# A list-scheduled transformer block: other latencies in the plan, and the mixer's x loaded earlier

## The chip, the cores and the metric

One Trainium2 chip, all eight NeuronCores. Each core computes one sequence of the batch with the same program. The metric is the device time of the slowest core, in microseconds. A program on all eight cores sometimes runs in a slower state, in which one die (cores 0 to 3 or 4 to 7), or both, is granted a lower TensorE clock.

## The reference

```python
def reference(x, c, ...):                       # x (8, 4096, 1024), c (8, 1024), float32
    mod = silu(c) @ w_mod + b_mod               # 9 modulation vectors a sequence
    h = ada_rmsnorm(x, g_ffn1, sh1, sc1)
    x = x + 0.5 * gt1 * swiglu_ffn(h)           # FFN 1: 1024 -> 2 x 2816 -> 1024
    h = ada_rmsnorm(x, g_mix, sh2, sc2)
    u_val, u_gate, u_x, u_y = split(h @ w_in)   # 4 x 512 channels
    y_conv = silu(layernorm(causal_conv31(u_val * sigmoid(u_gate))))
    y_rnn  = gelu(u_y) * rg_lru(causal_conv4(u_x))      # linear recurrence along the sequence
    x = x + gt2 * (concat(y_conv, y_rnn) @ w_out)
    h = ada_rmsnorm(x, g_ffn2, sh3, sc3)
    x = x + 0.5 * gt3 * swiglu_ffn(h)           # FFN 2
    return ada_rmsnorm(x, g_final, f_shift, f_scale)
```

## The kernel before

The sequence is cut into eight tiles of 512 tokens. The first 900 us run FFN 1, in four pairs of tiles. The rest runs mixer and FFN 2 tile by tile, and x goes through memory between the two phases (`xmid`). The instructions are not written in the order in which they run: every operation is added to a list with an estimated duration, a priority and its dependences, and a list scheduler (a greedy simulation on the host) decides the order on each engine, and which buffer each value takes. The program is then emitted in that order. The real semaphore waits come from the dependences, so a wrong estimate can't make the result wrong; it only makes the order a worse one.

The parts that matter here, with cuts marked:

```python
DMA_LAT = 2.0
SEM_LAT = 0.08
# ... schedule(): of the ready operations, the one of best priority that can start now ...
            else:                                  # a DMA
                c = max(s + dur, chan[0]) + op.nbytes
                chan[0] = c
                op.end = c + DMA_LAT               # when the plan thinks that it has landed
        else:
            op.end = s + sw + dur + SEM_LAT        # when the plan lets a dependent one start
# ...
        for q in op.succ:
            q.ready = max(q.ready, op.end if op in q.deps else s)
# ...
        def mix_ffn2(t):
            P.prio = 1000 + 10 * t if t else MIX0
            gate_op = (last_in, anchors[-2][1])[t] if t < 2 else ffn_anchor[t - 2]
            xs = load_x(xm_dr, t, after=(gate_op,) * 8)        # issued when gate_op starts
            hb = norm(xs, ...)                                 # row statistics: matmuls with "ones"
            # ... the four channel groups of the recurrent branch, on VectorE:
                    tsc(b, ux[c][:, 0:T], ...)                 # short convolution, tap 0
                    for k in range(1, 4):
                        stt(b, ux[c][:, k:k + T], ..., b, ...) # taps 1 to 3: each needs the last
            # ... gated linear unit: VectorE frees the PSUM bank of gv
                        stt(ub_t[...], s, 1.0, bv, ALU.add, ALU.mult, ...)
            # ... gate matmuls (need free banks), convolution, output projection w_out ...
            for j in range(FC):                                # FFN 2, 22 slabs of w2i
                slab = load_slab("w2i", j, False)
                ops = ffn_in(slab, [hb2], [hid], j)
            ffn_anchor[t] = ops[-1]                            # x of tile t + 2 is gated on this
            # ... FFN out; for tile 0 its w2o weights are cast to bf16 on first use:
                    slabs = [load_slab("w2o", 3 * q + s, t == 0 and cs.start == 0) for s in range(3)]
```

On VectorE and ScalarE the emitted program waits on the engine's own semaphore too, where an instruction needs the result of an earlier one of the same engine.

## Time and profile before

| what | value | where it is read |
|---|---|---|
| time | 2409.84 us median of 3 (2408.78 to 2412.9) | device times |
| span of the cores | 2386.8 to 2405.7 us | spans of all cores |
| TensorE (PE) busy, slowest core | 2318.5 us, 96% | the page, part 1 |
| PE idle, 61 us to the end of the matmuls | about 24 us | gaps in PE's timeline |

The page of the kernel before: first the busy time, share and number of instructions of each engine, then the chain of work that ended last, by engine.

```profile
PE 2318.5 (96%) x11346; PEld 1110.4 (46%) x11346; DVE 1183.6 (49%) x2019; ACT 931.4 (39%) x1394; POOL 111.2 (5%) x213
...
PE 87%; DMA 6%; ACT 3%; DVE 2%; issue 2%; SPq 1%; ACTq 0%; DVEq 0%; POOLq 0%
```

PE, busy 96% of the span, is the bound, so only its idle time and its granted clock can be won. Who PE waits for (view of the waits, engine PE; microseconds in total, times, longest; waits at the start and for weights left out):

```profile
PE ps L443 <- DVE sb_h L423: 37.0, 15, 12.4
...
PE ps L443 <- DVE sb_c L409: 4.3, 6, 0.8
...
PE ps L443 <- DVE sb_ub L419: 0.5, 1, 0.5
```

Of the 37.0 us behind `DVE sb_h`, which are the row statistics' inputs, some 19 us lie at the start of the program and 3.1 us near 216 us, where pair 1 waits for its x; 7.2 us are these two waits of tile 2's mixer (PE's timeline; start, duration, instruction, and in brackets the idle time before it and what ended it):

```profile
1190.42 0.59 PE L443 MATMUL ps<-sb_h,sb_ones 128*128 128x512 bf16 x1 [4.95 <-DVE sb_h L423]
...
1195.80 0.59 PE L443 MATMUL ps<-sb_h,sb_ones 128*128 128x512 bf16 x1 [2.23 <-DVE sb_h L423]
```

The clock falls with it: the record of core 0 has it at 0.5 for 10.2 us from 1189.2 us. Two stretches of 20 us of the windows view (the length; busy time and number for PE, weight loads, DVE, ACT, POOL; then PEclk, the granted clock; DMA share; GB/s):

```profile
1180.00:1200.00 20.00, 12.81 (x45) 4.87 (x44) 7.64 (x13) 8.68 (x13) 0.53 (x1) 0.74 0.97 282
1240.00:1260.00 20.00, 19.82 (x127) 12.17 (x126) 18.26 (x33) 16.74 (x28) 0.58 (x2) 1.00 1.02 228
```

In the first, PE is granted 0.74 of its clock. And the x loads of the mixer are waited for (view of the tile `xmid`, 1100 to 2200 us):

```profile
L450 SPq DMA_DIRECT2D sb_c<-xmid x48: 319/325/2065, 1178.3 to 2062.9; - x48
...
who waited for it (us, times):
  ACT sb_c L401: 35.1, 13
...
DMA to landing us min/median/max: 3.8/5.4/11.2
```

### The profile page before, as it was taken

The numbers are of one execution on the slowest core, as the hardware profiler recorded it, in microseconds if no ns is written. First come the engines' busy times: TensorE is split into PE (matmuls) and PEld (weight loads), VectorE is DVE, ScalarE is ACT, GpSimd is POOL, SyncE is SP. The second block draws the span as 40 slices with busy tenths as digits, with TensorE's granted clock in tenths as the row PEclk, the third lists the DMA queues.
The fourth block names the chain that finished last, engine by engine and source line by source line (L and its number), as shares of the span: only waits on it lengthen the run. The fifth ranks groups of instructions, "written<-read, shape, count | busy, mean of one in ns | idle before, by whom it ended". The sixth has DMA issues, their size and how long they took to land.

```text
span 2405.7 us, 35029 instructions; the slowest of 8 cores (2386.8 to 2405.7 us)
## 1 busy us (share of the span) xinstructions
PE 2318.5 (96%) x11346; PEld 1110.4 (46%) x11346; DVE 1183.6 (49%) x2019; ACT 931.4 (39%) x1394; POOL 111.2 (5%) x213
## 2 busy tenths in 40 slices
PE   1999999999999999999899999999999999999997
PEld 0444444444444445454354454454454454454446
DVE  6334133523352337585285385484484584574223
ACT  3214011401131116466265365364364364374222
POOL 0010100010010000000000000000000000000000
PEclk9999999999999999999999999999999999999999
DMA  9999599679867766464976555555555555555455
GB/s 274 226 210 240 176 218 220 166 197 221 218 173 188 187 178 206 153 214 149 225 187 221 189 180 188 187 181 185 191 177 191 186 183 185 186 182 188 162 184 184
DMA packets 135106, 466.64 MB, mean 194 GB/s; under 512 B 16368, under 2 KB 18544, under 8 KB 134256
## 3 DMA queue, kind: packets, MB, share of 16 engines
q1 hardware_dynamic: 117216, 386.54, 49.7%
q0 software_dynamic: 17712, 77.87, 17.3%
q8 instruction: 95, 1.56, 0.3%
q14 instruction: 83, 0.68, 0.1%
HBM read 453.07 MB, written 79.69 MB: 221 GB/s over the span
## 4 chain that ended last, share of the span: by engine, by line
PE 87%; DMA 6%; ACT 3%; DVE 2%; issue 2%; SPq 1%; ACTq 0%; DVEq 0%; POOLq 0%
PE ps L443 87%; DMA sb_c<-x 2%; ACT sb_c L401 2%; DMA sb_c<-xmid 2%; SPq L450 1%; DMA sb_slab<-wmod 1%; DVE sb_c L423 1%; DMA sb_slab<-w1i 0%; DVE sb_c L749 0%; DVE sb_c L409 0%; ACT L401 0%; DVE sb_h L423 0%; DVE sb_c L419 0%; DVE sb_ub L419 0%; DVE sb_c L429 0%
## 5 line engine op out<-in xcount | busy, mean ns | idle before, releaser
L443 PE MATMUL ps<-sb_h,sb_slab 128*128 128x512 bf16 (+1 forms) x10160 | 2178.2, 376 | 31.8 <-ACT sb_h L401 28.9
L443 PEld LDWEIGHTS ps<-sb_h,sb_slab 128*128 128x128 bf16 x10160 | 995.9, 98 | 1195.9 <-issue 44.6
L423 DVE TENSOR_TENSOR sb_h<-ps,sb_c 128x512 bf16<-128x512 f32 x352 | 241.4, 691 | 769.4 <-PE ps L443 708.6
L401 ACT ACTIVATE sb_c<-ps 128x512 f32<-128x512 f32 x400 | 236.5, 596 | 868.0 <-PE ps L443 864.5
L423 DVE TENSOR_TENSOR sb_c<-sb_c 128x512 f32<-128x512 f32 (+1 forms) x492 | 308.8, 672 | 115.6 <-ACT sb_c L401 113.0
L401 ACT ACTIVATE sb_c<-sb_c 128x512 f32<-128x512 f32 (+1 forms) x329 | 198.5, 616 | 263.0 <-DVE sb_c L419 183.3
L401 ACT ACT_TABLE_LOAD x106 | 136.0, 1283 | 224.7 <-PE ps L443 202.4
L419 DVE SCALAR_TENSOR_TENSOR sb_c<-ps,sb_gth,sb_c 128x512 f32<-128x512 f32 (+1 forms) x136 | 96.7, 717 | 212.0 <-PE ps L443 211.6
L401 ACT ACTIVATE sb_h<-sb_c,sb_modv,sb_gs 128x512 bf16<-128x512 f32 x151 | 108.9, 801 | 38.5 <-DVE sb_modv L423 24.9
L443 PE MATMUL ps<-sb_ub,sb_slab 128*128 128x256 bf16 x1024 | 115.0, 273 | 4.9 <-DVE sb_c L409 4.3
L443 PEld LDWEIGHTS ps<-sb_ub,sb_slab 128*128 128x128 bf16 x1024 | 99.5, 98 | 22.1 <-issue 8.7
L500 DVE SCALAR_TENSOR_TENSOR sb_slab<-sb_slab,sb_crow 128x1024 f32<-128x1024 f32 x88 | 107.1, 1217 | 3.4 <-DMA sb_slab<-wmod 2.4
L450 POOL DMA_DIRECT2D y<-sb_c x56 | 30.3, 542 | 1012.9 <-ACT sb_c L401 864.1
L423 DVE TENSOR_TENSOR sb_h<-sb_c 128x512 bf16<-128x512 f32 (+1 forms) x98 | 65.8, 678 | 21.8 <-ACT sb_c L401 19.6
L419 DVE SCALAR_TENSOR_TENSOR sb_c<-sb_ux,sb_vecs,sb_c 128x512 f32<-128x512 f32 x96 | 69.6, 746 | 1.7
L443 PE MATMUL ps<-sb_h,sb_ones 128*128 128x512 bf16 (+1 forms) x98 | 34.4, 382 | 37.3 <-DVE sb_h L423 37.0
L419 DVE SCALAR_TENSOR_TENSOR sb_c<-ps,sb_modv,sb_c 128x512 f32<-128x512 f32 x64 | 47.9, 749 | 31.0 <-PE ps L443 31.0
L419 DVE SCALAR_TENSOR_TENSOR sb_ub<-sb_c,ps 64x256 bf16<-64x256 f32 x128 | 53.8, 420 | 15.1 <-PE ps L443 11.6
L450 POOL DMA_DIRECT2D xmid<-sb_c x64 | 35.0, 547 | 361.6 <-DVE sb_c L419 357.8
L401 ACT ACTIVATE sb_c<-sb_c,sb_lam 128x512 f32<-128x512 f32 x64 | 50.0, 821 | 0.5
L409 DVE TENSOR_SCALAR sb_c<-ps,sb_vecs 64x256 f32<-64x256 f32 x85 | 40.7, 484 | 8.9 <-ACT sb_c L401 4.7
L401 ACT ACTIVATE sb_c<-sb_c,sb_modv,sb_gs 128x512 f32<-128x512 f32 (+1 forms) x65 | 43.6, 751 | 1.2 <-DVE sb_c L423 1.2
(50 smaller groups left out, 454.8 us busy)
## 6 DMA issues: line engine op xcount, KB each, us to landing
sb_slab<-b_w2i SPq DMA_DIRECT2D x176, 512.0 KB, 3.8
sb_slab<-b_w2o SPq DMA_DIRECT2D x96, 512.0 KB, 4.0
sb_slab<-wmod SPq DMA_DIRECT2D x88, 512.0 KB, 8.0
sb_slab<-b_w1i SPq DMA_DIRECT2D x66, 512.0 KB, 8.4
sb_slab<-b_win SPq DMA_DIRECT2D x64, 512.0 KB, 4.4
sb_slab<-b_dcw SPq DMA_DIRECT2D x64, 512.0 KB, 3.8
sb_slab<-b_w1o SPq DMA_DIRECT2D x36, 512.0 KB, 5.8
sb_c<-x SPq DMA_DIRECT2D x64, 256.0 KB, 11.2
```

What stands on the lines that cost most here:

```text
L401: return A("ACT", dur, lambda: (lambda o, i: (lambda h: [h.activation(out=o, in_=i, func=func, bias=bias, scale=scale)]))(out(), in_()), r ...
L409: f = lambda: (lambda o, a: (lambda h: [h.tensor_scalar(out=o, in0=a, scalar1=s1, scalar2=s2, op0=op0, op1=op1)]))(out(), in0())
L419: return A("DVE", dur, lambda: (lambda o, a, b: (lambda h: [h.scalar_tensor_tensor(out=o, in0=a, scalar=scalar, in1=b, op0=op0, op1=op1)]) ...
L423: return A("DVE", dur, lambda: (lambda o, a, b: (lambda h: [h.tensor_tensor(out=o, in0=a, in1=b, op=op)]))(out(), in0(), in1()), reads, wr ...
L443: return [h.matmul(o, lhsT=l, rhs=r, start=(first and i == 0), stop=(last and i == n - 1)) for i, (l, r) in enumerate(pr)]
L450: lambda: (lambda o, i: (lambda h: [h.dma_start(out=o, in_=i)]))(out(), in_()),
L500: return lambda h: [h.scalar_tensor_tensor(out=w, in0=w, scalar=1.0, in1=crow.ap, op0=ALU.mult, op1=ALU.mult, accum_out=o)]
```

## The change

Its intent: plan with a longer semaphore latency between engines (0.2 us) and almost none on one engine (0.02 us), plan the mixer's x with 8 us of latency, and issue its load from the 13th of the 22 FFN-in slabs of two tiles back instead of the last one.

```diff
-SEM_LAT = 0.08
+SEM_LAT = 0.2
...
-                op.end = c + DMA_LAT
+                op.end = c + op.lat                       # DMA_LAT unless given
...
-            q.ready = max(q.ready, op.end if op in q.deps else s)
+            t = s if op not in q.deps else op.end - SEM_LAT + 0.02 if op.on == q.eng and not op.nbytes and q.alt is None else op.end
+            q.ready = max(q.ready, t)
...
-            xs = load_x(xm_dr, t, after=(gate_op,) * 8)
+            xs = load_x(xm_dr, t, after=(gate_op,) * 8, lat=8.0)
...
                 ops = ffn_in(slab, [hb2], [hid], j)
-            ffn_anchor[t] = ops[-1]
+                if j == 12:
+                    ffn_anchor[t] = ops[-1]
```

(The rest of the diff passes `lat` through.) No arithmetic is added or taken away.

More of the change, by code (lines that the diff above doesn't have):

```diff
@@ L159, in res @@
         return self.fres if self.pool is None else self.pool.res[self.slot]
+DMA_LAT = 2.0
 class Op:
     __slots__ = ("eng", "dur", "fn", "reads", "writes", "prio", "tset", "deps", "succ", "ndep", "ready",
-                 "idx", "nbytes", "sem", "slab", "end", "after", "sync", "tok", "alt", "on")
+                 "idx", "nbytes", "sem", "slab", "end", "after", "sync", "tok", "alt", "on", "lat")
     def __init__(self):
@@ L176, in __init__, with add @@
         self.prio = 0
-    def add(self, eng, dur, fn, reads=(), writes=(), tset=None, nbytes=0, sem=None, slab=None, after=(), prio=None, sync=(), alt=None):
+    def add(self, eng, dur, fn, reads=(), writes=(), tset=None, nbytes=0, sem=None, slab=None, after=(), prio=None, sync=(), alt=None, lat=DMA_LAT):
         op = Op()
+        op.lat = lat
         op.alt = alt
@@ L207 @@
 D_CAST, D_SLAB, D_CHUNK, D_PREP = 2.7, 1.65, 0.85, 4.6
-DMA_LAT = 2.0
-SEM_LAT = 0.08
+SEM_LAT = 0.2
 SWITCH = 1.4
@@ L446, in mms, with dma @@
             return A("PE", mm_us(n, cols), f, reads, [bank], prio=prio)
-        def dma(q, out, in_, nbytes, sem, reads, writes, slab=None, after=(), prio=None, sync=()):
+        def dma(q, out, in_, nbytes, sem, reads, writes, slab=None, after=(), prio=None, sync=(), lat=DMA_LAT):
             return A(q, 0.06 if q == "SP" else 0.3,
                      lambda: (lambda o, i: (lambda h: [h.dma_start(out=o, in_=i)]))(out(), in_()),
-                     reads, writes, nbytes=nbytes, sem=sem, slab=slab, after=after, prio=prio, sync=sync)
+                     reads, writes, nbytes=nbytes, sem=sem, slab=slab, after=after, prio=prio, sync=sync, lat=lat)
         dr = lambda d, r: d[r * 128:(r + 1) * 128, :]
@@ L523, in build_program, with load_x @@
         tsc(k_(bah.ap), k_(V[:, V_BA:V_BA + 8]), 0.5, None, ALU.mult, None, [vecs], [bah], dur=0.17)
-        def load_x(src, t, prio=None, after=(None,) * 8):
+        def load_x(src, t, prio=None, after=(None,) * 8, lat=DMA_LAT):
             xs = []
@@ L530, in load_x @@
                 d = src[t][f]
-                dma("SP", lambda b=b: b.ap, lambda d=d: d.ap, D_CHUNK, slot_sem(b), [d], [b], prio=prio, after=(after[f],))
+                dma("SP", lambda b=b: b.ap, lambda d=d: d.ap, D_CHUNK, slot_sem(b), [d], [b], prio=prio, after=(after[f],), lat=lat)
                 xs.append(b)
```

## The prediction

> **What bounds the kernel.** TensorE: the page gives PE 2318.5 us busy of 2405.7 (96%), and the chain that ended last is 87% matmuls. On core 0 about 87 us are not matmul. By the PE timeline's gaps, 50 us lie before 61 us (startup loads), 3.1 us at 216 us, 13 us after the last matmul; only 20 us follow 900 us, 2.2 us of them in the tail.
>
> These are of three kinds. (a) At 1185 to 1196 us PE waits 4.95 and 2.23 us for the row statistics of tile 2's mixer; the chain shows an 11.2 us xmid landing just before. The x loads are issued only when the last FFN-in matmul of tile 0 ends, and the plan counts 2 us of latency. The clock record is at 0.5 for 10.2 us there: 5 us more lost. [...] (4.95 us gap, half clock; 0.8 us gaps leave it alone). (b) The same wait for tiles 3 to 7: 0.74, 0.63, 1.62, 0.25, 1.40 us, after landings of 5 to 6 us. (c) Five waits of 0.8 us before a depthwise-convolution group, for a VectorE copy (L409).
>
> **What the change does.** No instruction is added or removed; it reorders. The gate of the mixer's x moves from the 22nd to the 13th FFN-in slab of two tiles back: [...]about 31 us earlier. Landings measured 5 to 11 us, so x is there before PE needs it. This should remove (a) with its clock dip and (b). The longer semaphore latency separates producer and consumer by about 0.1 us more and may remove half of (c). Cost: eight of 40 f32 buffers are held some 30 us longer, so three tiles' x (24) live beside mixer temporaries.
>
> **On the critical path.** All of it, since PE is the bound. Core 0: 7.2 + 5.1 (clock) + 4.6 + about 3 = 20 us. Core 7 (2404.4 us): about 4.1 + 3.4 + 4.8 + 3 = 15. Core 5 (2398.9): about 2.6 + 1.7 + 1.4 + 3 = 9, so it ends near 2390. The metric is the slowest core, so the gain is the fall of the maximum, about 15 us. The startup and the 216 us gap (7.1 us and a 10 us dip on core 7) stay. Predicted 2394 us, range 2383 to 2406; faster by over 2% 0.01, within 2% 0.97, slower by over 2% 0.02.
>
> **What would show it.** Right: in the PE waits "DVE sb_h" falls from 37.0 us by 10 or so; no gap over 1 us before ones-matmuls between 1100 and 2100 us; no half clock near 1190 us on any core; in the queue's timeline the xmid loads are issued about 30 us before FFN-in ends and leave the chain. Wrong: gaps reappear for buffers, slabs or VectorE at the mixer's start; or they stay because ACT and DVE, not the landing, make the statistics late.
>
> **What would make it wrong.** The list scheduler is greedy: another latency reshuffles everything, including the first 900 us where x already arrives late (40 us landing near 177 us). [...] Buffer shortage could serialize a tile's mixer with the FFN before it.

The traces show no such border: in before a gap of 2.15 us (core 3, 216 us) was followed by half clock and one of 3.27 us (core 6, 1186 us) was not (counts in the last section). The forecast: its sums are 20, 15 and 9 us on cores 0, 7 and 5, its 5.1 us of clock are half of the 10.2 us recorded at half clock, and 2394 us is about 15 us less than before.

## The result, and the profile after

After: 2409.19 us median of 4 (2408.39, 2408.56, 2409.83, and one run of 2859.16, in which cores 0 to 3 were granted a clock of 0.82; the three fast runs alone have a median of 2408.56). Before, in the same set: 2409.31 us (2407.95 to 2412.9). The ratio is 0.9996, 95% interval 0.9976 to 1.0016: the same. Ratios here and below are the mean time of one kernel's fast runs over that of the other's of the same rounds, so they are not quite the ratio of the medians quoted beside them. Executions in which one die ran at a lower clock are left out of the means.

The page of the kernel after:

```profile
PE 2304.0 (96%) x11139; PEld 1111.0 (46%) x11346; DVE 1193.3 (50%) x2010; ACT 934.0 (39%) x1399; POOL 111.3 (5%) x213
...
PE 84%; DVE 6%; DMA 5%; issue 3%; ACT 2%; SPq 0%; DVEq 0%; ACTq 0%; POOLq 0%
```

This trace lacks 207 of the 11346 matmul records on that core, so PE's busy time is not compared. The gaps are: other cores of the same run lack no record, and the gaps between weight loads, of which no record is missing, show them too.

What the change aimed at, it did. The same view of `xmid`:

```profile
L454 SPq DMA_DIRECT2D sb_c<-xmid x48: 319/325/682, 1144.9 to 2032.5; - x48
...
who waited for it (us, times):
...
DMA to landing us min/median/max: 4.2/5.5/8.0
```

The loads are issued about 30 us earlier (tile 2's at 1144.9 instead of 1178.3 us), land as late as before after their issue (5.5 us against 5.4 us), and no engine of any core waits for them any more between 1100 and 2200 us. Of the marks that the prediction set, two are met: the longest gap before a ones-matmul between 1100 and 2100 us is 0.56 us on all cores (before: 4.95 us on core 0), and no core has half clock near 1190 us. The third nearly is (`DVE sb_h` falls by 7.5 us, as the wait near 216 us grew from 3.1 to 6.8 us on core 0). So what failed is not there. The clock at 1180 us is full again, and low at another place:

```profile
1180.00:1200.00 20.00, 18.82 (x89) 8.75 (x90) 17.59 (x37) 6.64 (x13) 0.00 (x0) 1.00 0.49 159
1240.00:1260.00 20.00, 15.70 (x62) 6.53 (x62) 8.98 (x13) 4.42 (x7) 1.59 (x3) 0.83 1.02 230
```

The waits of PE:

```profile
PE ps L447 <- DVE sb_h L427: 29.5, 13, 12.7
PE ps L447 <- DVE sb_ub L423: 8.6, 8, 1.3
...
PE ps L447 <- DMA sb_slab<-b_wout: 4.2, 1, 4.2
```

Of these, `DMA sb_slab<-b_wout` is new, and `DVE sb_ub` has grown from one wait of 0.5 us. The first is one wait of 4.25 us, where tile 1's output projection needs its last slab of weights:

```profile
1239.75 9.01 PE L447 MATMUL ps<-sb_h,sb_slab 128*128 128x512 bf16 x40
1253.01 3.57 PE L447 MATMUL ps<-sb_h,sb_slab 128*128 128x512 bf16 x8 [4.25 <-DMA sb_slab<-b_wout]
```

That slab's load was issued at 1225.1 us and landed at 1252.8: 27.6 us, beside twelve casts of w2o that tile 0's first FFN-out does in these same 65 us. And the wait for `sb_ub` comes once a tile, between the gate matmuls, which need the PSUM banks that VectorE's `sb_ub` instructions free:

```profile
1378.44 1.46 PE L447 MATMUL ps<-sb_h,sb_gates 128*128 128x512 bf16 x5
1381.23 0.59 PE L447 MATMUL ps<-sb_h,sb_gates 128*128 128x512 bf16 x2 [1.32 <-DVE sb_ub L423]
```

The whole account: PE's gaps of over 0.12 us from the matmul records by stretch, as the mean of the eight cores. The stretches are: the FFN 1 pairs (100 to 900 us), the first mixer (900 to 1140), the collision with the w2o casts (1140 to 1300), and five steady tiles (1300 to 2200).

| gaps, us | 100-900 | 900-1140 | 1140-1300 | 1300-2200 |
|---|---|---|---|---|
| before | 3.2 | 0.7 | 5.2 | 7.0 |
| after | 5.8 | 3.1 | 3.3 | 8.0 |

After the last matmul, 14.4 us follow instead of 12.8. So from 1140 to 1300 us 1.9 us were saved, and everything else got worse by 2.6, 2.4, 1.0 and 1.6 us; the mean span of the cores rose from 2397.6 to 2400.8 us. (The sum is 5.7 us and the span rose by 3.2; the rest was not followed up.) As the matmuls are the same, the question is what made the new waits: the early mixer, or the latencies.

### The profile page after: what moved, and what is told of

It is laid out like the page before. It is cut to its first block, busy times and chain, and to the rows that moved or that the text cites. A ratio compares the mean times of both kernels' runs of the same rounds, so it can differ in the third digit from the quotient of the medians.

```text
span 2407.0 us, 34746 instructions; the slowest of 8 cores (2395.7 to 2407.0 us)
## 1 busy us (share of the span) xinstructions
PE 2304.0 (96%) x11139; PEld 1111.0 (46%) x11346; DVE 1193.3 (50%) x2010; ACT 934.0 (39%) x1399; POOL 111.3 (5%) x213
## 4 chain that ended last, share of the span: by engine, by line
PE 84%; DVE 6%; DMA 5%; issue 3%; ACT 2%; SPq 0%; DVEq 0%; ACTq 0%; POOLq 0%
PE ps L447 84%; DMA sb_c<-x 2%; DVE sb_c L423 1%; DMA sb_slab<-b_wout 1%; ACT sb_c L405 1%; ACT L405 1%; DVE sb_ub L423 1%; DVE sb_c L753 1%; DVE sb_c L413 1%; DMA sb_slab<-w2o 1%; DVE sb_c L427 1%; DMA sb_slab<-wmod 1%; DVE sb_h L427 1%; DMA sb_slab<-w1i 0%; DVE sb_c L433 0%
## 5 line engine op out<-in xcount | busy, mean ns | idle before, releaser
L405 ACT ACTIVATE sb_h<-sb_c,sb_modv,sb_gs 128x512 bf16<-128x512 f32 x162 | 117.7, 806 | 32.6 <-DVE sb_modv L427 26.8
```

The costliest lines, as they stand in the source:

```text
L405: return A("ACT", dur, lambda: (lambda o, i: (lambda h: [h.activation(out=o, in_=i, func=func, bias=bias, scale=scale)]))(out(), in_()), r ...
```

## The experiments

Twelve runs were made, in three sets (e1 to e4, e5 to e8, e9 to e12), each set on one chip with the kernel before beside it. The three chips are different ones; which chip the result was measured on is not recorded. Before was profiled only in the set of the result. All gave a correct result.

Theory 1: the early x gains (some 6 us, by the gaps), and the latency part gives it back. Theory 2: the early x itself only moves the collision and crowds the mixer, and the latency part is neutral.

### e1: the early x without the latency part

```diff
 (against after)
-SEM_LAT = 0.2
+SEM_LAT = 0.08
-            t = s if op not in q.deps else op.end - SEM_LAT + 0.02 if ... else op.end
+            t = s if op not in q.deps else op.end
```

> The change without its latency part: semaphore latency back to 0.08, no special rule for the same engine; x still gated on the 13th FFN-in slab and planned with 8 us. Theory 1 (the early x gains some 6 us, and the reshuffle by the new semaphore latency gives it back): about 2402 us, ratio to before 0.996 to 0.998, and the gaps plus clock loss between 100 and 900 us back at the 5.3 us mean of the eight cores that before has (after: 9.0). Theory 2 (the early x only moves the collision with the w2o casts of tile 0 from the xmid loads to the wout loads, and the latency part is neutral): about 2409 us, with the wait for wout near 1250 us still there.

Measured: 2401.13 us median of five fast runs against 2419.59 us before (ten fast runs) on that chip; ratio 0.9927 [0.9908, 0.9945]. The gaps from 1300 to 2200 us fall to 2.1 us, and PE waits on core 0 there for nothing but this:

```profile
PE ps L447 <- DVE sb_c L413: 1.9, 5, 0.5
```

The latency part is not neutral, so theory 2 is out; its other half stands, as every core of e1 still waits for wout near 1250 us (0.3 to 4.4 us). The gain is larger than expected, 18.5 us by the medians. The trace does not account for all of it: against the one trace of before, gaps and half clock between 100 and 2200 us fall by some 7.5 us in the mean, and before itself took 10 us longer on this chip than in the set of the result.

### e2: the latency part alone

```diff
 (against after)
-            xs = load_x(xm_dr, t, after=(gate_op,) * 8, lat=8.0)
+            xs = load_x(xm_dr, t, after=(gate_op,) * 8)
-                if j == 12:
-                    ffn_anchor[t] = ops[-1]
+            ffn_anchor[t] = ops[-1]
```

> The latency part alone: semaphore latency 0.2 us, 0.02 on the same engine, x gated at the end of FFN-in and planned with 2 us as before. Theory 1: slower than before by 4 to 8 us, about 2415 us, with 9 us lost between 100 and 900 us, 2 us more at 900 to 1140 us, and the wait for xmid near 1185 us unchanged (about 7 us mean). Theory 2: 2409 us, same as before within 2 us.

Measured: ratio 1.0035 [1.0014, 1.0057] to before, 2428.19 us median of six fast runs against 2419.59. Slower by itself, by 8.6 us, as theory 1 said, and everywhere: gaps of 6.2, 4.3, 7.5 and 9.9 us in the four stretches.

### e3: after, with x planned at 2 us

```diff
 (against after)
-            xs = load_x(xm_dr, t, after=(gate_op,) * 8, lat=8.0)
+            xs = load_x(xm_dr, t, after=(gate_op,) * 8)
```

> After, with the mixer's x planned at 2 us again instead of 8. If the 8 us matters for more than the first tiles, the statistics of tiles 2 to 7 are again asked for before x has landed (5 to 8 us), and waits of 1 us or more before ones-matmuls come back, 3 to 6 us in all: about 2414 us. If the early gate alone is what counts: 2409 us, and no such wait, as the greedy plan has FFN-in work to fill.

Measured: ratio 0.9985 [0.9963, 1.0008]. Waits of 0.5 to 1.8 us before ones-matmuls did come back on the slowest core (core 6), as feared, but the gaps from 1300 to 2200 us are 6.2 us in the mean, not more than after's 8.0. The 8 us in the plan is no part of the loss, and by this run no clear gain either.

### e4: after, with the w2o casts during tile 0's FFN-in

```diff
 (against after)
                 ops = ffn_in(slab, [hb2], [hid], j)
+                if t == 0 and j < 12:          # cast one w2o slab, memory to memory
+                    src, d = dr(w_src["w2o"], j), scr["w2o"][j]
+                    dma("PL", ..., D_PREP, ..., [], [d, psem[j % 8]], sync=(ops[-1],), prio=450)
...
-load_slab("w2o", 3 * q + s, t == 0 and cs.start == 0)
+load_slab("w2o", 3 * q + s, False)
```

> After, with the w2o weights cast to bf16 during tile 0's FFN-in (12 casts from memory to memory) instead of on their first use in tile 0's FFN-out. If the wait for wout near 1250 us (2.2 us gap and 1.1 us clock loss in the mean, 4.3 + 3.4 us on the slowest core) is the queueing behind those casts (28 us landing), it goes and the run takes about 2404 us, ratio to after about 0.998; the wout landing near 1225 us falls from 27.6 us to under 8. If the wait is for slabs or for the order of the queue, it stays and the time is 2409 us.

Measured: slower, ratio 1.0052 [1.0028, 1.0075] to before (four fast runs, four slow). Cores 4 to 7 (clock 0.985 to 0.988) have 15.1 us of gaps from 1140 to 1300 us. The waits of PE on core 7 in that stretch:

```profile
PE ps L447 <- ACT sb_h L405: 6.1, 1, 6.1
PE ps L447 <- DMA sb_slab<-b_w2i: 5.6, 1, 5.6
```

The expectation missed. The wait for wout went, but one cast per slab of FFN-in (16 matmuls, about 3.5 us at the 0.216 us from start to start in the trace of before) was too much: on core 7 the DMA engines were busy for 0.98 or more of the time from 1090 to 1180 us, and the w2i slabs of the very stage that hides the casts took up to 37.6 us to land. The experiment moved the collision and says nothing yet on whether the casts can be hidden elsewhere; e7 does.

### e5 and e6: the two halves of the latency part

What in the latency part loses? In after's trace VectorE waits for its own last result 338 times a core between 900 and 2300 us, 35.4 us in all; in e1's 165 times, 10.8 us. In after the wait takes 0.104 us (median), and the plan counted 0.02. So theory A: the rule for the same engine makes the plan put dependent VectorE instructions one right behind the other. Theory B: the 0.2 us between engines loses.

e5 keeps the 0.2 us and drops the rule:

```diff
 (against after)
-            t = s if op not in q.deps else op.end - SEM_LAT + 0.02 if ... else op.end
+            t = s if op not in q.deps else op.end
```

> Early x, semaphore latency 0.2 us everywhere, but without the rule that an engine's own result costs it only 0.02 us. In after VectorE waits 338 times a core (900 to 2300 us) for its own last result, 35 us in all, at a median of 0.104 us; in the run with the early x alone 165 times and 11 us. Theory A (the 0.02 us rule is what loses: the plan puts dependent VectorE instructions back to back, and VectorE feeds the banks that PE waits for at the gates): about 2401 us or the ratio of the early x alone (0.993), VectorE's own waits at 11 us or less, no wait at the gates. Theory B (0.2 us between engines is what loses): as after, ratio near 1.000.

e6 keeps the rule and plans 0.08 us between engines:

```diff
 (against after)
-SEM_LAT = 0.2
+SEM_LAT = 0.08
-  ... op.end - SEM_LAT + 0.02 if op.on == q.eng ...
+  ... op.end - 0.06 if op.on == q.eng ...
```

> Early x, semaphore latency 0.08 us between engines as before, with the 0.02 us rule for the same engine. Theory A: as after, ratio near 1.000, VectorE's own waits near 34 us and a PE wait of about 1.3 us per tile at the gates. Theory B: as the early x alone, ratio 0.993.

This chip was disturbed: in many runs that count as fast, pairs of cores have a mean clock of about 0.98, and these runs are 15 to 30 us longer. The profiles of e7 and e8 show why: there such cores were granted 0.81 for some 160 us. The ratios of all fast runs are therefore wide: 0.997 [0.992, 1.002] and 0.996 [0.991, 1.002], and decide nothing. Of the runs in which every core kept a mean clock of 0.99 or more, before took 2415.1 us (median of four), e5 2404.8 and 2405.0, e6 2410.6 and 2410.8. Two runs of each were picked after the fact, so these times only lean to theory A. The profiled runs of e5 and e6 are among them, and their traces decide it. The waits of PE on core 0 of e5 from 1300 to 2200 us:

```profile
PE ps L447 <- DVE sb_h L427: 1.1, 5, 0.3
```

The same view of e6:

```profile
PE ps L447 <- DVE sb_ub L423: 5.2, 5, 1.3
PE ps L447 <- DVE sb_c L413: 3.7, 10, 0.5
```

Gaps in that stretch, mean of the cores: 1.1 us in e5, 9.4 us in e6. VectorE's waits for itself: 10.0 us and 35.7 us. Theory A holds; with the rule the five waits at the gates are there, with 0.2 us between engines as with 0.08. (The rule is for every engine, not VectorE alone; see e9.)

### e7: e1, with the w2o casts spread over the pair phase

```diff
 (against e1)
-prep = [(nm, r) for nm in ("win", "dcw", "wout", "w2i") for r in ...]
+prep = [(nm, r) for nm in ("win", "dcw", "wout", "w2i", "w2o") for r in ...]
...
-load_slab("w2o", 3 * q + s, t == 0 and cs.start == 0)
+load_slab("w2o", 3 * q + s, False)
```

> The early x alone, and the 12 w2o casts put at the end of the list of weight casts that is spread over pairs 1 to 3 (one cast per 11 us instead of per 14), instead of on first use. If the casts were too dense in the run that put them into tile 0's FFN-in (one per 3.4 us), here the wait for wout near 1245 us (3.1 us gap and about 2 us clock loss in the mean) goes and nothing comes back: ratio to the early x alone 0.997 to 0.999, about 2397 us. If the pair phase has no room for them, x or w1i lands late between 220 and 900 us and the loss there grows from 4 us by 3 us or more.

The one undisturbed run took 2397.81 us, against 2415.1 before; the ratio of all fast runs is 0.992 [0.986, 0.998]. The gaps from 1140 to 1300 us fall from e1's 3.1 us to 0.3 us. All that PE waits for there on core 0:

```profile
PE ps L447 <- DVE sb_c L413: 0.3, 1, 0.3
```

Tile 1's wout slabs land 3.3 to 5.2 us after issue; in e1 it was 13.1 to 26.6 us. So the wait was the casts' queueing, and the pair phase has the room that FFN-in had not. Whether x in the pair phase pays for it could not be told apart from the chip's disturbance.

### e8: e1, with x planned at 2 us

> The early x alone, planned with 2 us of latency as in before instead of 8. With the semaphore latency of after the 8 us was worth nothing in the mean of the cores. If so here too: ratio to the early x alone within 0.001 of 1. If the plan now asks for statistics before x has landed: waits of 0.5 to 2 us before ones-matmuls at each tile, 5 us in all, ratio 1.002.

```diff
 (against e1)
-            xs = load_x(xm_dr, t, after=(gate_op,) * 8, lat=8.0)
+            xs = load_x(xm_dr, t, after=(gate_op,) * 8)
```

Undisturbed runs: 2398.7 and 2398.9 us, against 2415.1 before. In the trace three cores (0, 3 and 6) have about 5 us of gaps from 1300 to 2200 us and the other five 1.9 to 2.7; e1's all have 1.9 to 2.7. e7, which plans 8 us and ran on this chip, has 1.9 to 2.7 us on all cores too. So the 8 us helps a core whose x comes late; no difference in time is claimed, as e1 ran on another chip and e7 moves the casts as well. The early gate is what counts.

### e9 and e10: the change with one constant corrected, and the change again

```diff
 (e9, against after; e10 is after itself)
-  ... op.end - SEM_LAT + 0.02 if op.on == q.eng ...
+  ... op.end - SEM_LAT + 0.1 if op.on == q.eng ...
```

> The change as it is, with one constant corrected: an engine's own result costs the next instruction 0.10 us in the plan, as the trace measures on VectorE (median 0.104 us), instead of 0.02. If the one constant is the cause: the gaps of 1300 to 2200 us fall from 8.0 us (mean of the cores) to 1 to 3, VectorE's own waits between 900 and 2300 us from 35 us to about 10, and undisturbed runs take 2398 to 2405 us, 0.3% less than after on the same chip.

> The change itself again, unaltered, as the control on the same chip: ratio to before 0.998 to 1.001, gaps of 8.0 us between 1300 and 2200 us.

Measured on one chip: e9 2394.12 us (2393.08 to 2396.0, three fast runs), e10 2412.76 us (2411.9 to 2414.82, five). To before (2419.2): 0.989 [0.985, 0.993] and 0.997 [0.994, 1.000]. A change of 0.08 us in one constant is worth 18.6 us here, more than e9's expectation (it is 0.8% less than after; 0.3% was expected). The mean spans of the cores are 2387.7 and 2405.7 us; of these 18.0 us, 8.0 come from the gaps of 1300 to 2200 us (8.0 to 0.0), 3.0 from 900 to 1140 (3.1 to 0.1), 3.4 from 1140 to 1300 and 2.9 from 100 to 900 (both with their half-clock stretches; the last section counts the gaps that these followed).

How the constant does it is to be seen on VectorE. The recurrent branch has four short convolutions of four taps each, each tap needing the one before. After, on core 0, in order of time:

```profile
1360.41 0.55 DVE L433 TENSOR_SCALAR sb_c<-sb_ux,sb_vecs 128x512 f32<-128x512 f32 x1 [1.54 <-ACT sb_ux L405]
1361.07 2.46 DVE L423 SCALAR_TENSOR_TENSOR sb_c<-sb_ux,sb_vecs,sb_c 128x512 f32<-128x512 f32 x3
...
1364.04 0.54 DVE L433 TENSOR_SCALAR sb_c<-sb_ux,sb_vecs 128x512 f32<-128x512 f32 x1
1364.69 2.46 DVE L423 SCALAR_TENSOR_TENSOR sb_c<-sb_ux,sb_vecs,sb_c 128x512 f32<-128x512 f32 x3
...
1375.26 7.78 DVE L423 SCALAR_TENSOR_TENSOR sb_ub<-sb_c,ps 64x256 bf16<-64x256 f32 x16
```

Three taps take 2.46 us, 0.856 us from start to start (the median of all such pairs; 0.75 us and a wait of 0.104); the convolutions stand one behind the other, and only at 1375.26 us do the sixteen `sb_ub` instructions start that PE needs at 1378 us. The same stage with the constant at 0.10:

```profile
1349.94 0.54 DVE L433 TENSOR_SCALAR sb_c<-sb_ux,sb_vecs 128x512 f32<-128x512 f32 x1
1350.39 1.41 DVE L423 SCALAR_TENSOR_TENSOR sb_c<-sb_ux,sb_vecs,sb_c 128x512 f32<-128x512 f32 x2
...
1358.62 0.41 DVE L423 SCALAR_TENSOR_TENSOR sb_ub<-sb_c,ps 64x256 bf16<-64x256 f32 x1
...
1360.70 4.03 DVE L423 SCALAR_TENSOR_TENSOR sb_ub<-sb_c,ps 64x256 bf16<-64x256 f32 x9
1366.06 1.78 DVE L423 SCALAR_TENSOR_TENSOR sb_ub<-sb_c,ps 64x256 bf16<-64x256 f32 x4 [1.33 <-PE ps L447]
```

Here the plan believes in the wait, so it puts a tap of another convolution into it. Interleaved taps start 0.663 us apart (1.41 us for two, the second's full 0.75 included), overlapping by some 0.08 us; the first `sb_ub` comes at 1358.62 us, before the convolutions have ended, and VectorE now waits for PE (1.33 us at 1366.06) instead of PE for it. The groups of instructions tell it over the five tiles (1300 to 2200 us, core 0; busy time, mean ns of one, then the idle time just before them and what ended it). The kernel before:

```profile
L419 DVE SCALAR_TENSOR_TENSOR sb_c<-sb_ux,sb_vecs,sb_c 128x512 f32<-128x512 f32 x60 | 43.5, 747 | 1.0
...
L419 DVE SCALAR_TENSOR_TENSOR sb_ub<-sb_c,ps 64x256 bf16<-64x256 f32 x80 | 33.6, 420 | 9.5 <-PE ps L443 7.3
```

The kernel after:

```profile
L423 DVE SCALAR_TENSOR_TENSOR sb_c<-sb_ux,sb_vecs,sb_c 128x512 f32<-128x512 f32 x60 | 45.1, 751 | 6.6 <-DVE sb_c L423 0.5
...
L423 DVE SCALAR_TENSOR_TENSOR sb_ub<-sb_c,ps 64x256 bf16<-64x256 f32 x80 | 33.6, 420 | 5.6 <-DVE sb_ub L423 0.5
```

e9:

```profile
L423 DVE SCALAR_TENSOR_TENSOR sb_c<-sb_ux,sb_vecs,sb_c 128x512 f32<-128x512 f32 x60 | 43.5, 745 | 1.1
L423 DVE SCALAR_TENSOR_TENSOR sb_ub<-sb_c,ps 64x256 bf16<-64x256 f32 x80 | 33.6, 420 | 9.4 <-PE ps L447 7.2
```

In after, the 60 taps have 6.6 us of idle time before them instead of 1.0, and the `sb_ub` group is never held up by PE, because it is VectorE that is late. The groups of PE in the same stretch, with the same columns, of the kernel before:

```profile
L443 PE MATMUL ps<-sb_ub,sb_slab 128*128 128x256 bf16 x640 | 71.8, 273 | 4.0 <-DVE sb_c L409 4.0
L443 PE MATMUL ps<-sb_h,sb_ones 128*128 128x512 bf16 x50 | 16.5, 378 | 4.7 <-DVE sb_h L423 4.6
L443 PE MATMUL ps<-sb_h,sb_gates 128*128 128x512 bf16 x40 | 11.1, 378 | 0.2
```

Of the kernel after:

```profile
L447 PE MATMUL ps<-sb_h,sb_ones 128*128 128x512 bf16 x50 | 18.9, 379 | 2.7 <-DVE sb_h L427 2.4
L447 PE MATMUL ps<-sb_h,sb_gates 128*128 128x512 bf16 x35 | 10.0, 378 | 5.9 <-DVE sb_ub L423 5.6
```

Of e9:

```profile
L447 PE MATMUL ps<-sb_h,sb_ones 128*128 128x512 bf16 x50 | 17.3, 379 | 0.0
L447 PE MATMUL ps<-sb_h,sb_gates 128*128 128x512 bf16 x35 | 9.5, 379 | 0.3
```

Before, PE lost 4.0 us at the convolutions and 4.6 at the statistics; after, 2.4 at the statistics and 5.6 at the gates; in e9 none of them waits. (Some matmul records are missing in the last two, x35 for 40; the weight loads, all recorded, show the same, and in e9 no pause of over 0.3 us.)

Why 0.02 us reorders the taps and 0.08 does not can be read in a line of the scheduler that the change left alone:

```python
                now = s <= et[e] + 0.03        # s: earliest start; et[e]: when engine e is free
                key = (0 if now else 1, op.prio + (sw and 0.5) if now else s + sw, op.idx)
```

An operation that has to wait 0.02 us still counts as ready now and is taken by its priority; one that waits 0.08, 0.10 or 0.20 us does not, and another goes first. The traces split there. In the six with the rule at 0.02 us (after, e2, e3, e4, e6, e10) every pair of taps that follow each other from 1300 to 2200 us has the wait (320 pairs on eight cores, 304 in e4); in the other eight, planned with 0.08 (before, e1, e7, e8, e11, e12), 0.10 (e9) or 0.20 us (e5), 40 of 160 have it. No run tried a value between 0.02 and 0.08, so that 0.03 is the border is read from the source and not measured.

Two limits. e9 is a new plan as a whole, so 18.6 us is the worth of this pair of plans. And the rule is for every engine, and e9 corrects it for all: ScalarE's waits for its own results go the same way (9.1 us in after and e10, 2.5 in e9, 4.2 in before, 900 to 2300 us, mean of cores 0 to 3). The waits at the gates are VectorE's by the trace; what ScalarE's share of the loss is was not tested.

### e11 and e12: a faster version

e7, with x of the next pair gated on the 2nd FFN-in slab of the pair before (e11) or on the 1st (e12) instead of the 4th. The order of PE, VectorE, ScalarE and GpSimd is the same as in e7; only that of the SyncE queue changes.

```diff
 (against e7)
-                if j >= 3:
+                if j >= 1:          # e12: j >= 0
                     next_in.append(ops[-1])
```

> Early x, old latencies, w2o casts in the list of the pair phase, and the x of the next pair gated two FFN-in slabs earlier (on the 2nd slab instead of the 4th), which alters the order of the SyncE queue alone. If the last x of pair 1, which lands 29 to 40 us after its issue near 222 us, is late because it is issued late: it lands 13 us earlier, the loss between 100 and 900 us falls from about 8 us to about 2, and undisturbed runs take 2390 to 2396 us. If the transfers of that stretch are bound by bandwidth alone, the wait moves to the w1i or w1o casts and the time stays at about 2398 us.

> The same with x gated three slabs earlier instead of two: as the one before, within 2 us, if two slabs were enough; slower if the casts of w1i now come late between 60 and 215 us.

Measured beside e9 and e10: e11 2393.55 us, ratio to before 0.988 [0.984, 0.992]; e12 2388.98 us (2385.01 to 2389.05, three fast runs), 0.986 [0.982, 0.990]. The gaps from 100 to 900 us are 3.6 us and 1.2 us (e10: 8.6). The last x of pair 1 lands at 220.0 and 216.0 us on core 0, in e7 at 228.0. It still takes about 40 us from issue to landing. e11's expectation was half met (8 us earlier instead of 13, and 3.6 us of gaps left where about 2 were expected), and two slabs were not enough; by the ratios alone, whose intervals overlap, e12 is not shown to be faster than e11. The fastest and the slowest core of e12, from the view of the cores:

```profile
core 1: 2379.8 us, clock 0.996
core 2: 2387.4 us, clock 0.997
```

e12 beats both kernels: 1.25% less than before by the medians (2419.2 us), 1.0% less than after (2412.76 us).

### The account over all runs

Gaps of PE in us as the mean of the eight cores, and VectorE's waits for its own result (900 to 2300 us, mean of cores 0 to 3). e4 is left out (slow).

| run | 100-900 | 900-1140 | 1140-1300 | 1300-2200 | VectorE's own waits |
|---|---|---|---|---|---|
| before | 3.2 | 0.7 | 5.2 | 7.0 | 10.5 |
| after | 5.8 | 3.1 | 3.3 | 8.0 | 35.4 |
| e1 early x alone | 3.9 | 0.5 | 3.1 | 2.1 | 10.8 |
| e2 latencies alone | 6.2 | 4.3 | 7.5 | 9.9 | 34.2 |
| e3 after, x at 2 us | 5.2 | 4.2 | 1.4 | 6.2 | 33.8 |
| e5 0.2 us, no rule | 8.4 | 0.1 | 3.1 | 1.1 | 10.0 |
| e6 0.08 us, rule | 8.8 | 5.1 | 1.7 | 9.4 | 35.7 |
| e7 e1 + casts in pair phase | 4.6 | 0.2 | 0.3 | 2.1 | 10.8 |
| e8 e1, x at 2 us | 6.4 | 0.6 | 0.7 | 3.4 | 13.0 |
| e9 after, 0.10 us | 7.0 | 0.1 | 1.4 | 0.0 | 10.2 |
| e10 after again | 8.6 | 3.1 | 3.7 | 8.0 | 35.4 |
| e11 e7, x at slab 2 | 3.6 | 0.2 | 0.3 | 2.1 | 10.8 |
| e12 e7, x at slab 1 | 1.2 | 0.2 | 0.3 | 2.1 | 10.8 |

The last column splits the table: every run with the rule at 0.02 us has 33 us or more there, at least 3 us of gaps at the first mixer and 6 us or more in the steady tiles; every run with an early x and without it has 13 us or so at most, 0.6 us or less, and 3.4 us or less. The first column does not follow it. It hangs on when pair 1's x lands, and both chip and order move it. One kernel has 5.8 us in one set and 8.6 in another (after and e10). And until about 870 us the traces of before, e1 and e8 have the same order of instructions on every engine, and those of after, e2, e3 and e10 have another in common: on the chip of e1 to e3 the old order has 3.9 us, the new one 6.2 and 5.2; in the set of the result it is 3.2 and 5.8.

## Why the prediction was wrong, point by point

- **PE is the bound and only its gaps can be won**: right. What the traces show of later gains and losses is gaps and stretches of half clock (in before, on core 0: a gap of 4.95 us at 1185 us and a clock of 0.5 for 10.2 us).
- **x arrives about 30 us earlier and is waited for no more** (a, b): right in the trace of after (35.1 us of waits for xmid gone; 9 slabs of 16 matmuls, which start 0.216 us apart in the trace of before, make 31 us). And it is worth at least what was predicted: e1, which does this alone, gains 18.5 us on its chip where 15 were expected for the whole change, and e8 16.3 us (two picked runs).
- **"The longer semaphore latency separates producer and consumer by about 0.1 us more and may remove half of (c)"**: this is the step that failed. It costed only one half of the latency part, the 0.2 us between engines, and left out the other, the 0.02 us on the same engine. That half was not small: e9 against e10 puts 18.6 us on it, as much as the early x gains; the whole latency part without the early x costs 8.6 us (e2). The prediction booked a gain of about 3 us for it (half of (c), whose five waits sum to 4.0 us, would be 2). The waits of kind (c) did go, but waits for `sb_ub` at the gates and for the statistics took their place, 8.0 us from 1300 to 2200 us instead of 7.0.
- The number that would have told was in the trace of before: VectorE's wait for its own result, 0.104 us, can be read there between dependent taps that stand next to each other. I looked at latencies between engines and not at that.
- **"The startup and the 216 us gap stay"**: the startup did; the gaps from 100 to 900 us, of which this is the largest, grew from 3.2 to 5.8 us in the mean (on core 0 the gap itself from 3.1 to 6.8 us), and the half clock there from 2.1 to 3.2 us. That is the reshuffle that the prediction named as a risk. A new long wait came too, near 1250 us, on four of the eight cores (2.0 to 4.3 us), as the earlier mixer put tile 1's wout loads among the w2o casts that had delayed xmid before. This one is the price of the early x, as e1 has it too.
- **"The metric is the slowest core"**: right in kind. Of after's eight cores four have the wait near 1250 us, and these four are the slowest: 2402.8 to 2407.0 us against 2395.7 to 2397.8.
- What stays open: why after was 0.3% faster than before in one set and even in another; why before took 6 to 10 us longer in the later sets (it was not profiled there), so that the gains in time against it are larger than the gaps account for; and what ScalarE's part in the latency rule is.

## What to carry to other kernels

Where a list scheduler orders the program, its constants are part of the kernel: measure each latency in a trace, the engine's wait for its own result too, before setting it, and look at the tolerances that it is compared with. Here the dangerous side was the small one: at 0.02 us, under the scheduler's 0.03, the plan filled a wait with nothing and the engine paid it every time, while 0.08, 0.10 and 0.20 us all kept the taps interleaved, for a measured wait of 0.104. When a change has two parts and the time does not move, run each part alone before believing that neither does anything.

## What else the traces show

- Interleaved 128x512 taps on VectorE start 0.663 us apart, taps that wait for each other's semaphore 0.856 us (medians; before has both, 120 and 40 pairs on eight cores from 1300 to 2200 us). The wait costs 0.19 us each against the order that avoids it. From the end of one to the start of one that waits for it, it is 0.104 us.
- Nothing starts on VectorE in the 0.104 us in which the next tap waits (320 pairs in after), and in e1, e7, e11 and e12, whose plans differ in DMAs alone, its 2018 records on core 0 stand in one and the same order though x lands at other times.
- Half clock after gaps of PE: in the thirteen traces that are not slow, of the gaps between 100 and 2300 us that did not begin at half clock, a half-clock stretch began in the gap or within 1 us after it for 11 of 18 of 2.0 to 2.5 us, 7 of 17 of 2.5 to 3.5 us and 95 of 97 of over 3.5 us, but for 2 of 361 from 0.8 to 2.0 us (both of 0.93 us, 1 us after another gap of 1.2). All but one of the stretches that followed last about 3.4, 6.8 or 10.2 us.
- Eight cores with PE 96% busy for 2400 us were granted 0.978 to 0.998 in the runs that count as fast, three quarters of the values 0.992 or more. Lower clocks were granted too: 0.817 to 0.819 in the mean on cores 0 to 3 in the slow run of after, and about 0.81 for some 160 us on pairs of cores in e7 (2 and 3, 6 and 7: 0.81 to 0.82 in the mean from 60 to 240 us, where the other four have 0.95 to 0.97) and e8 (6 and 7, with 0.982 in the mean of the run).
- Of the loads issued by SyncE, 256 KB chunks of x landed after 5.4 us (median, 1100 to 2200 us), but in before after 24.6 to 40.0 us where they were issued between 154 and 194 us, and 512 KB of wout after 27.6 us among casts in after. The DMA share alone does not tell them apart: in after, at a share of 1.02 between issue and landing, one chunk of x took 9.8 us (issued at 89.9 us) and another 39.6 us (at 173.7 us).
